# 8 KB runs in the expert weight loads, and the next expert's token count read to registers in mid-expert

## The chip, the cores and the metric

The kernel runs on one core of one Trainium2 chip. The metric is the device time of one execution in microseconds (us). All times below are of that one core; a profiled execution also leaves a span, from its first instruction to its last.

## The reference

One layer of an encoder on 256 tokens of width 1024, in float32: an attention and recurrent mixer with input and output projections, then a mixture of 32 experts of which each token uses 4, then a final norm. Nearly all the weights are the experts': three matrices of 1024 by 1024 each, 12 MB per expert, 403 MB in all. Cut to the experts:

```python
logits = (xf @ w_router + b_router)
top_v, top_i = lax.top_k(logits, 4)
gates = jax.nn.softmax(top_v)
# for each expert e, for the tokens that chose it:
g = xb @ w_gate[e] + b_gate[e]
u = xb @ w_up[e] + b_up[e]
g = jnp.minimum(g, 7.0)
u = jnp.clip(u, -7.0, 7.0)
y = ((u + 1.0) * (g * sigmoid(1.702 * g))) @ w_down[e] + b_down[e]
out[token] += gate * y
```

## The kernel before, in words

The front part (attention, recurrence, output projection, router) takes the first 149 us. It leaves for every token and expert a position in that expert's list (`pos`), a gate, and for every expert the number of its tokens (`cnti`).

Then a loop over 32 experts, written out. One expert handles up to 64 of its tokens in a block: its x columns are gathered and transposed to `xT`, `ffn1` multiplies them by `w_gate` (into PSUM tile `pg`) and `w_up` (`pu`), the activation follows on VectorE (DVE) and ScalarE (ACT), `h_trans` transposes the hidden activations, and `ffn2` multiplies by `w_down` (`pu`). With only 64 rows, two matmuls (`h` or `q` of 0 and 1) run side by side in the two column halves of TensorE. Gather of the next expert and scatter of the last pair lie between these stages. TensorE's instruction stream is called PE, its weight loads PEld, and what its sequencer handles alone PEq.

Should an expert have more than 64 tokens, `overflow` runs further blocks (`ov_block`) ahead of the normal one, nested up to three deep, each behind a branch on the count. The count must be in a register of PE, DVE and ACT for that: `load_cnt(e)` (line 994) reads it with `TENSOR_LOAD`, and on PE also computes and issues a `BRANCH_PREFETCH_HINT` for the branch. In the loop it stands right behind the branch of expert e and reads the count of e + 1. Where an `If` is skipped, each engine's sequencer runs an `EVENT_SEMAPHORE` (line 928), which on PE waits until all matmuls ahead have ended.

Weights come in chunks of 1 MB: 256 rows of a matrix, two rows (k = 0, 1) for each of 128 partitions, 4 KB each from two places 512 KB apart. Four chunks make a matrix, twelve an expert. `prefetch` (line 165) issues them all from SyncE (SP, line 173) in the order of use into a ring of 21 slots (`RING`), so SP runs ahead until it has to wait for a slot. A chunk's slot comes free when the last matmul on it has ended.

Of the kernel before, what the change touches and what calls it, by code (L numbers as in the profile page):

```python
# [18 lines left out]
ET = mybir.EngineType  # L19
# [4 lines left out]
KC = D // 128  # L24
# [15 lines left out]
def rope_table():  # L40
# [8 lines left out]


COLS = [("norm1_g", 8), ("conv_w", 16), ("conv_b", 4), ("lru_ba", 8), ("lru_bi", 8), ("lru_lam", 8),
        ("norm2_g", 8), ("attn_out_g", 4), ("lru_out_g", 4)]
OFF = {n: sum(c for _, c in COLS[:i]) for i, (n, _) in enumerate(COLS)}
NCOL = sum(c for _, c in COLS)


def packs(a):

    cols = np.concatenate([np.asarray(a[n]).reshape(c, 128) for n, c in COLS]).T
    rope = rope_table().reshape(NT, 128, 2 * HD).transpose(1, 0, 2).reshape(128, -1)  # L60
    heads = [np.broadcast_to(np.asarray(a[n]).reshape(1, HD), (128, HD)) for n in ("q_norm_g", "k_norm_g")]
    lru = [np.asarray(a[n])[0].reshape(2, LC, 2, 64, 64).transpose(2, 3, 0, 1, 4).reshape(128, -1)
           for n in ("lru_wa", "lru_wi")]
    wr = np.asarray(a["w_router"])[0].reshape(KC, 128, E).transpose(1, 0, 2).reshape(128, -1)
    br = np.broadcast_to(np.asarray(a["b_router"]).reshape(1, E), (128, E))
    return {"pack_a": np.ascontiguousarray(cols),
            "pack_b": np.ascontiguousarray(np.concatenate([rope] + heads + lru, 1)),
            "pack_c": np.ascontiguousarray(np.concatenate([wr, br], 1))}


def bc(ap, shape):
    return ap.to_broadcast(shape)


def body(ctx, tc, A, out):
    nc = tc.nc
    V, S, G, PE = nc.vector, nc.scalar, nc.gpsimd, nc.tensor
# [80 lines left out]


    w_out_d = A["w_out"][0].rearrange("(c k p) n -> c p k n", k=2, p=128)  # L160
    srcs = [A[n][0].rearrange("e (c k p) n -> e c p k n", k=2, p=128) for n in ("w_gate", "w_up", "w_down")]
    plan = [("o", 0, c) for c in (0, 1, 2, 3)] + [(m, e, c) for e in range(E) for m in range(3) for c in range(4)]
    loaded = {}

# [681 lines left out]
def experts(tc, A, out, g):  # L846
# [5 lines left out]
    with ExitStack() as ctx:  # L852
# [3 lines left out]
        Y = [wk.tile([128, 512], F32, name=f"Y{d}") for d in range(2)]  # L856
        xo = wk.tile([128, KC, 64], F32, name="xo")
        gTo = wk.tile([128, NT, 128], F32, name="gTo")
        n2 = bc(pcols("norm2_g", KC).rearrange("p (h c) -> p c h", h=2)[:, :, :, None], [128, 4, 2, 64])

        ssf = wk.tile([128, NT, 2], F32, name="ssf")

# [9 lines left out]
        def gather(sl):  # L872
# [6 lines left out]
            S.activation(xr, p, AF.Copy)  # L879
            return xr  # L880

        def gather_trans(xr, dst):
            p = ps([128, 4, 2, 64])
            for c in range(4):
                PE.transpose(p[:, c].rearrange("p a b -> p (a b)"), xr[:, c * 128:(c + 1) * 128], ident)  # L885
            V.tensor_tensor(dst.rearrange("p (h c) s -> p c h s", h=2), p, n2, OP.mult)  # L886

        def ffn1(w, xT, e, which, tag="pu"):
# [10 lines left out]
        def act_gate(p, gp):  # L899
            sg = wk.tile([128, 512], F32, name="sg", tag="sg")  # L900
            V.tensor_scalar(gp, p, LIMIT, None, op0=OP.min)  # L901
            S.activation(sg, gp, AF.Sigmoid, scale=ALPHA)  # L902
            V.tensor_tensor(gp, gp, sg, OP.mult)
# [6 lines left out]
        def h_trans(h, hT):  # L910
            p = ps([128, 4, 128])
            for c in range(4):
                PE.transpose(p[:, c, :], h[:, c * 128:(c + 1) * 128], ident)  # L913
            S.activation(hT, p.rearrange("p a b -> p (a b)"), AF.Copy)

        def ffn2(w, hT, flip):
# [8 lines left out]

        def overflow(cnt, e, w, b=1):

            with tc.If(cnt > 64 * b, preferred_fallthrough_block=True, label=f"ov{e}" if b == 1 else None):  # L928
                ov_block(e, b, *w)
                if b < 3:  # L930
                    overflow(cnt, e, w, b + 1)
# [61 lines left out]

        def load_cnt(e):
            c = nc.values_load(cnti[:, e:e + 1], engines=(ET.PE, ET.DVE, ET.Activation), min_val=0, max_val=T)
            tc.mark_branch_hint_location(f"ov{e}", (c + 191) >> 8, engines=(ET.PE,))
            return c

        def ov_block(e, b, wg, wu, wd):
            gather_trans(gather(select(e, b)), xo)  # L1000
# [10 lines left out]
        xr = gather(sl)  # L1011
# [5 lines left out]
        for e in range(E):  # L1017
            last = e == E - 1
            wg, wu, wd = weights(0, e), weights(1, e), weights(2, e)
            overflow(cnt, e, (wg, wu, wd))  # L1020
            if not last:
                cnt = load_cnt(e + 1)
            gp = wk.tile([128, 512], F32, name="gp")
            if e >= E - 2:
                gd = one_pick(e, 0, "gd")
            elif e % 2 == 1:
                gd = combine(e)
            if not last:
                sl = select(e + 1, 0)
            pg = ffn1(wg, xT, e, 0, "pg")  # L1030
            act_gate(pg, gp)
            if last:
                one_scatter(g0, Y[0], False, (0,))
                one_scatter(g0, Y[0], False, (1,), (0,))
                g1 = wk.tile([128, NT, 2, 128], F32, name="gT", tag="gT")[:, :, 0]
                one_weights(g1, gd)
            act_up(ffn1(wu, xT, e, 1), gp)
            if e == E - 2:
                g1 = wk.tile([128, NT, 128], F32, name="g1")
                one_weights(g1, gd)  # L1040
            elif e % 2 == 1 and not last:
                gT = pair_weights(gd)
            if not last:
                xr = gather(sl)
            hT = wk.tile([128, 512], F32, name="gd", tag="gd")
            h_trans(gp, hT)
            if last:
                one_scatter(g0, Y[0], False, (1,), (1,))
            else:
                xT = wk.tile([128, KC, 64], F32, name="xT")  # L1050
                gather_trans(xr, xT)
            if e % 2 == 0 and e > 0:
                pair_scatter(gT, False)
            if e == 2:
                add_b_down()
            if e < E - 2:
                py = ffn2(wd, hT, e % 2)
                for q in range(2):
                    S.activation(Y[q ^ (e % 2)][q * 64:q * 64 + 64, :], py[q * 64:q * 64 + 64, :], AF.Copy)  # L1059
            else:  # L1060
                S.activation(Y[e % 2], ffn2(wd, hT, 0), AF.Copy)  # L1061
            if e == E - 2:
                g0 = g1
                fgs = slot([128, NT, D])
                fgb, fgrow = fgs[:, 0], fgs[0:KC, 1, 0:128]
                nc.gpsimd.dma_start(fgrow, A["final_g"].rearrange("(n p) -> n p", p=128))  # L1066
                for h in range(2):
                    p = ps([128, 4, 128])
                    for c in range(4):
                        k = h * 4 + c  # L1070
                        PE.matmul(p[:, c, :], lhsT=bc(ident[0:KC, k:k + 1], [KC, 128]), rhs=fgrow,
                                  start=True, stop=True)
                    V.tensor_copy(fgb[:, h * 512:(h + 1) * 512], p.rearrange("p a b -> p (a b)"))
# [46 lines left out]
```

## Time and profile before

| | |
|---|---|
| time, median of 3 runs | 1143.39 us (1140.66 to 1144.08) |
| profiled execution, its time | 1146.21 us |
| its span | 1144.5 us |
| PE busy | 1040.8 us, 91% of the span |
| HBM read | 416.54 MB, 365 GB/s over the span |
| granted TensorE clock, mean | 0.970 of full speed |

The profiled execution took 1.7 us beyond its span, and 2.8 us more than the median of the runs. PE busy counts every matmul from start to modelled end, and matmuls overlap, so 91% says that PE seldom stood still, not that it ran at its peak. Both PE and the transfers from HBM are busy most of the time, so the averages alone don't tell which one sets the end.

### The profile page before, as it was taken

Reading aid. Unit: us, or ns where it says so; the run is one execution under the profiler, and the core shown is the slowest. Engines: PE = TensorE matmul, PEld = TensorE weight load, DVE = VectorE, ACT = ScalarE, POOL = GpSimd, SP = SyncE. Lnnn points to the kernel's source line nnn. Section 1 sums busy time; section 2 is a strip of 40 time slices with the busy share of each in tenths; the row PEclk is TensorE's granted clock in tenths of the full one; section 3 lists DMA queues with packets and bytes.
Section 4 is the critical chain, followed back from the end, with each engine's and each line's share of the span. In section 5 each row is a group of like instructions: output and inputs, shape, how many; then the busy total and the mean of one; then the engine's idle time right before and its main releaser. Section 6 shows DMA issues by size and latency. Waiting matters only on the chain. (4 is left out here: it accounts for less than half of the span.)

```text
span 1144.5 us, 12376 instructions
## 1 busy us (share of the span) xinstructions
PE 1040.8 (91%) x4886; PEld 413.1 (36%) x4886; DVE 277.0 (24%) x601; ACT 190.2 (17%) x341; POOL 67.0 (6%) x54
## 2 busy tenths in 40 slices
PE   7877989999899899987999999799999999999995
PEld 6664533333333333322333333233333333333331
DVE  8797412111112111210112121021211111212121
ACT  4745511111111111110011111011111111111112
POOL 5554200000000000000000000000000000000000
PEclk9889989999999999997999999899999999999998
DMA  9456769999999999996999999399999999999993
GB/s 322 188 200 251 284 249 403 409 408 409 408 409 408 409 408 409 408 409 243 391 408 408 409 408 409 139 394 410 407 409 408 408 408 409 408 409 408 408 409 147
DMA packets 114144, 419.14 MB, mean 366 GB/s; under 512 B 6664, under 2 KB 13968, under 8 KB 114032
## 3 DMA queue, kind: packets, MB, share of 16 engines
q1 hardware_dynamic: 113856, 417.21, 92.4%
q8 instruction: 74, 1.21, 0.4%
q0 software_dynamic: 176, 0.40, 0.1%
q14 instruction: 38, 0.31, 0.1%
HBM read 416.54 MB, written 1.05 MB: 365 GB/s over the span
## 5 line engine op out<-in xcount | busy, mean ns | idle before, releaser
L895 PE MATMUL pg<-w,xT 128*64 128x512 f32 x1024 | 234.3, 611 | 0.0
L922 PE MATMUL pu<-w,gd 128*64 128x512 f32 x1024 | 228.5, 599 | 0.0
L895 PE MATMUL pu<-w,xT 128*64 128x512 f32 x1024 | 225.4, 592 | 0.0
L895 PEld LDWEIGHTS pg<-w,xT 128*64 128x64 f32 x1024 | 78.0, 141 | 135.6 <-issue 131.5
L895 PEld LDWEIGHTS pu<-w,xT 128*64 128x64 f32 x1024 | 75.7, 137 | 138.0 <-issue 130.3
L922 PEld LDWEIGHTS pu<-w,gd 128*64 128x64 f32 x1024 | 71.1, 137 | 144.1 <-issue 136.7
L901 DVE TENSOR_SCALAR gp<-pg 128x512 f32<-128x512 f32 x32 | 22.1, 692 | 338.9 <-PE pg L895 338.9
L1059 ACT ACTIVATE Y<-pu 64x512 f32<-64x512 f32 x60 | 35.5, 592 | 271.9 <-PE pu L922 271.5
L902 ACT ACTIVATE sg<-gp 128x512 f32<-128x512 f32 x32 | 20.1, 629 | 287.8 <-DVE gp L901 287.8
L865 DVE TENSOR_SCALAR gd<-iota,pos,gates 128x64 f32<-128x64 f32 x128 | 30.1, 309 | 153.5 <-PEq L928 143.5
L907 DVE TENSOR_SCALAR sg<-pu 128x512 f32<-128x512 f32 x34 | 23.5, 692 | 161.0 <-PE pu L895 160.8
L876 PE MATMUL pt<-x,sr 128*64 128x512 f32 x256 | 61.3, 599 | 0.0
L891 PE MATMUL pg<-b,emask 96*64 96x512 bf16 x68 | 14.7, 427 | 49.4 <-issue 25.1
L973 PE MATMUL ps<-Y,gT 128*128 128x512 f32 x120 | 54.0, 592 | 0.0
L1066 POOL DMA_DIRECT2D w<-in_final_g_dram x1 | 0.5, 523 | 868.2 <-DMA w<-in_w_down_dram 868.2
L879 ACT ACTIVATE sg<-pt 128x512 f32<-128x512 f32 x34 | 20.3, 597 | 138.4 <-PE pt L876 138.4
L891 PEld LDWEIGHTS <-emask 96*64 96x64 bf16 x136 | 8.1, 109 | 85.7 <-issue 78.8
L886 DVE TENSOR_TENSOR xT<-pt,prm 128x512 f32<-128x512 f32 x32 | 22.1, 692 | 67.8 <-PE pt L885 67.8
L695 PE MATMUL ps<-w 128*128 128x512 f32 x64 | 30.2, 623 | 4.9 <-DVE w L571 4.9
L973 PEld LDWEIGHTS ps<-Y,gT 128*128 128x128 f32 x120 | 21.6, 190 | 21.5 <-issue 21.5
L885 PE MATMUL pt<-ident,sg 128*128 128x128 f32 x136 | 22.2, 286 | 6.4 <-ACT sg L879 6.3
L876 PEld LDWEIGHTS pt<-x,sr 128*64 128x64 f32 x256 | 17.2, 136 | 29.9 <-issue 25.4
(282 smaller groups left out, 768.3 us busy)
## 6 DMA issues: line engine op xcount, KB each, us to landing
w<-in_w_gate_dram SPq DMA_DIRECT2D x128, 1024.0 KB, 18.4
w<-in_w_up_dram SPq DMA_DIRECT2D x128, 1024.0 KB, 18.4
w<-in_w_down_dram SPq DMA_DIRECT2D x127, 1024.0 KB, 18.3
w<-in_w_in_dram SPq DMA_DIRECT2D x6, 1024.0 KB, 13.1
w<-in_w_out_dram SPq DMA_DIRECT2D x4, 1024.0 KB, 7.5
x<-in_x_dram SPq DMA_DIRECT2D x2, 512.0 KB, 3.9
w<-in_w_in_dram SPq DMA_DIRECT2D x2, 512.0 KB, 6.6
w<-in_w_down_dram SPq DMA_DIRECT2D x2, 512.0 KB, 17.6
```

The costliest lines, as they stand in the source:

```text
L695: PE.matmul(p, lhsT=mT[:, kk, t * 128:(t + 1) * 128], rhs=wo[kk // 2][:, kk % 2, d * 512:(d + 1) * 512], start=k == 0, stop=k == 3)
L865: V.tensor_scalar(dst[:, t], iota[:, b], pos[:, t, e:e + 1], weight[:, t], op0=OP.is_equal, op1=OP.mult)
L876: PE.matmul(p[h * 64:h * 64 + 64, :], lhsT=sl[:, t, :], rhs=x1[:, t, h * 512:(h + 1) * 512], start=t == 0, stop=t == NT - 1)
L885: PE.transpose(p[:, c].rearrange("p a b -> p (a b)"), xr[:, c * 128:(c + 1) * 128], ident)
L886: V.tensor_tensor(dst.rearrange("p (h c) s -> p c h s", h=2), p, n2, OP.mult)
L891: PE.matmul(p[h * 64:h * 64 + 64, :], lhsT=bc(emask[:, e:e + 1], [96, 64]), rhs=b3[:, which, h * 512:(h + 1) * 512], start=True, stop=False)
L895: PE.matmul(p[h * 64:h * 64 + 64, :], lhsT=xT[:, k, :], rhs=w[k // 2][:, k % 2, h * 512:(h + 1) * 512], start=False, stop=k == KC - 1)
L901: V.tensor_scalar(gp, p, LIMIT, None, op0=OP.min)
L907: V.tensor_scalar(u, p, LIMIT, -LIMIT, op0=OP.min, op1=OP.max)
L922: PE.matmul(p[q * 64:q * 64 + 64, :], lhsT=hT[:, c * 128 + hf * 64:c * 128 + hf * 64 + 64], rhs=w[j // 2][:, j % 2, d * 512:(d + 1) * 512] ...
L973: PE.matmul(acc[t][d], lhsT=gT[:, t, d, :], rhs=Y[d], start=False, stop=last)
L1059: S.activation(Y[q ^ (e % 2)][q * 64:q * 64 + 64, :], py[q * 64:q * 64 + 64, :], AF.Copy)
```

## The change

Two changes go together. First, the weight chunks of `w_gate`, `w_up` and `w_down` are cut so that one partition's two rows are neighbours in HBM: one run of 8 KB in place of two of 4 KB. Partition p of a chunk then holds rows 2p and 2p + 1, no longer p and 128 + p. So the transposes that feed these matmuls (`gather_trans`, `h_trans`) take every second column (`column_pairs`), and the norm's gains get a second copy in that order (`norm2_p`). Second, `load_cnt(e + 1)` moves behind the first `ffn1` of expert e. With it, each of the nested overflow branches gets a prefetch hint of its own, issued at the start of the block ahead of it; before, only the first had one.

```diff
 COLS = [...
-        ("norm2_g", 8), ("attn_out_g", 4), ("lru_out_g", 4)]
+        ("norm2_g", 8), ("attn_out_g", 4), ("lru_out_g", 4), ("norm2_p", 8)]
...
+    pairs = np.asarray(a["norm2_g"]).reshape(4, 128, 2).transpose(0, 2, 1)
...
-    srcs = [A[n][0].rearrange("e (c k p) n -> e c p k n", k=2, p=128) for n in ("w_gate", "w_up", "w_down")]
+    srcs = [A[n][0].rearrange("e (c p k) n -> e c p k n", k=2, p=128) for n in ("w_gate", "w_up", "w_down")]
...
+        def column_pairs(a, c):
+
+            return a[:, c // 2 * 256 + c % 2:(c // 2 + 1) * 256:2]
+
         def gather_trans(xr, dst):
...
-                PE.transpose(p[:, c].rearrange("p a b -> p (a b)"), xr[:, c * 128:(c + 1) * 128], ident)
+                PE.transpose(p[:, c].rearrange("p a b -> p (a b)"), column_pairs(xr, c), ident)
...
         def h_trans(h, hT):
...
-                PE.transpose(p[:, c, :], h[:, c * 128:(c + 1) * 128], ident)
+                PE.transpose(p[:, c, :], column_pairs(h, c), ident)
...
-            with tc.If(cnt > 64 * b, preferred_fallthrough_block=True, label=f"ov{e}" if b == 1 else None):
+            with tc.If(cnt > 64 * b, preferred_fallthrough_block=True, label=f"ov{e}_{b}"):
+                if b < 3:
+                    hint(cnt, e, b + 1)
                 ov_block(e, b, *w)
...
         def load_cnt(e):
             c = nc.values_load(cnti[:, e:e + 1], engines=(ET.PE, ET.DVE, ET.Activation), min_val=0, max_val=T)
-            tc.mark_branch_hint_location(f"ov{e}", (c + 191) >> 8, engines=(ET.PE,))
+            hint(c, e, 1)
             return c
+
+        def hint(c, e, b):
+
+            tc.mark_branch_hint_location(f"ov{e}_{b}", (c + 255 - 64 * b) >> 8, engines=(ET.PE,))
...
             overflow(cnt, e, (wg, wu, wd))
-            if not last:
-                cnt = load_cnt(e + 1)
...
             pg = ffn1(wg, xT, e, 0, "pg")
+            if not last:
+                cnt = load_cnt(e + 1)
             act_gate(pg, gp)
```

On PE, at the end of an expert's overflow branches, before the change (the rows `ISA` are register operations of the count and the hint; `pg` and `pu` are the first products):

```order
L928 UNCONDITIONAL_BRANCH x4
L995 TENSOR_LOAD cnti
L995 ISA x2
L996 ISA
L1116 BRANCH_PREFETCH_HINT
L891 LDWEIGHTS emask
L891 MATMUL pg<-b_78,emask 64x512
L891 LDWEIGHTS emask
L891 MATMUL pg<-b_78,emask 64x512
L895 MATMUL pg<-w,xT 64x512 x16
L891 LDWEIGHTS emask
L891 MATMUL pu<-b_78,emask 64x512
```

The same place with the change:

```order
L933 UNCONDITIONAL_BRANCH x4
L896 LDWEIGHTS emask
L896 MATMUL pg<-b_78,emask 64x512
L896 LDWEIGHTS emask
L896 MATMUL pg<-b_78,emask 64x512
L900 MATMUL pg<-w,xT 64x512 x16
L1002 TENSOR_LOAD cnti
L1002 ISA x2
L1008 ISA
L1127 BRANCH_PREFETCH_HINT
L896 LDWEIGHTS emask
L896 MATMUL pu<-b_78,emask 64x512
```

The load, its register operations and the hint have moved from ahead of the `pg` matmuls to behind them.

On PE, at the start of an overflow block, with the change:

```order
L927 MATMUL pu<-w,gd 64x512 x16
L933 COMPARE_AND_BRANCH
L1008 ISA
L1127 BRANCH_PREFETCH_HINT
L877 MATMUL pt<-x_68,sro 64x512 x4
L890 MATMUL pt<-ident,sg 128x128 x4
```

The two rows between the branch and the block's first matmul are new: the hint for the next nested branch.

On SP, the weight loads around one of the branches, before the change:

```order
L173 DMA w<-in_w_down_dram 128x2x1024 x4
L173 DMA w<-in_w_gate_dram 128x2x1024
L928 UNCONDITIONAL_BRANCH
L173 DMA w<-in_w_gate_dram 128x2x1024 x3
L173 DMA w<-in_w_up_dram 128x2x1024 x4
```

And with the change:

```order
L174 DMA w<-in_w_down_dram 128x2048 x4
L174 DMA w<-in_w_gate_dram 128x2048
L933 UNCONDITIONAL_BRANCH
L174 DMA w<-in_w_gate_dram 128x2048 x3
L174 DMA w<-in_w_up_dram 128x2048 x4
```

The order and number of loads is unchanged; each now names 128 runs of 2048 elements, where it named 256 of 1024.

## Rows read from the trace of the kernel before

**Rows 1.** The page: the span, and the DMA rate in 40 slices.

```profile
span 1144.5 us, 12376 instructions
...
GB/s 322 188 200 251 284 249 403 409 408 409 408 409 408 409 408 409 408 409 243 391 408 408 409 408 409 139 394 410 407 409 408 408 408 409 408 409 408 408 409 147
```

**Rows 2.** Busy by stretch (us, then busy by engine, clock, DMA share, GB/s): two experts.

```profile
563.60:589.90 26.30, 25.08 (x120) 8.83 (x120) 5.29 (x13) 3.44 (x7) 0.00 (x0) 1.00 1.02 410
589.90:619.00 29.10, 27.77 (x124) 9.86 (x124) 4.43 (x10) 3.00 (x6) 0.00 (x0) 1.00 1.03 408
```

**Rows 3.** SP in order of time, around the second overflow block.

```profile
709.29 35.10 SPq L173 DMA_DIRECT2D w<-in_w_down_dram  x3
742.31 3.80 SPq L173 DMA_DIRECT2D w<-in_w_down_dram  x3
```

**Rows 4.** PEld in order of time, expert 30, third and fourth chunk of w_up.

```profile
1084.34 0.15 PEld L895 LDWEIGHTS pu<-w,xT 128*64 128x64 f32 x2 [0.28 <-issue]
1085.26 0.20 PEld L895 LDWEIGHTS pu<-w,xT 128*64 128x64 f32 x4 [0.77 <-DMA w<-in_w_up_dram]
```

**Rows 5.** PE in order of time, the boundary before an even expert.

```profile
589.98 0.41 PE L891 MATMUL pg<-b,emask 96*64 96x512 bf16 x2 [1.11 <-PEq L928]
```

**Rows 6.** Sequencer instructions of lines 928, 995, 996, 1116: ns min/median/max.

```profile
L928 PEldq COMPARE_BRANCH  x36: 90/3364/6090, 144.4 to 1101.2; - x36
L928 PEldq EVENT_SEMAPHORE  x32: 51/51/51, 148.0 to 1103.3; - x32
L995 PEldq TENSOR_LOAD <-cnti x32: 302/306/493, 143.2 to 1071.8; - x32
L995 PEldq FUSED_REGOPS  x32: 157/157/171, 143.8 to 1072.2; - x32
L995 PEldq SEQ_ASSERT  x32: 18/18/24, 144.1 to 1072.4; - x32
L996 PEldq FUSED_REGOPS  x32: 59/59/65, 144.1 to 1072.5; - x32
L1116 PEldq BRANCH_PREFETCH_HINT  x32: 35/35/53, 144.3 to 1072.6; - x32
```

**Rows 7.** Line 891 from 149 to 739 us: pu's first matmul, sequencer's event.

```profile
L891 PE MATMUL pu<-b,emask x40: 381/382/383, 159.0 to 710.5; 96*64 96x512 bf16 x40
L891 PEldq EVENT_SEMAPHORE  x18: 51/51/51, 154.8 to 677.2; - x18
```

**Rows 8.** DMA from 742 to 1126 us: all packets, queue 1.

```profile
DMA packets 40065, 154.69 MB, mean 403 GB/s; under 512 B 2390, under 2 KB 2398, under 8 KB 40024
...
q1 hardware_dynamic: 39992, 154.13, 100.7%
```

**Rows 9.** DMA from 5 to 11 us, loads of 1 KB rows.

```profile
DMA packets 1974, 2.09 MB, mean 348 GB/s; under 512 B 48, under 2 KB 1936, under 8 KB 1974
...
q1 hardware_dynamic: 1974, 2.09, 104.1%
```

**Rows 10.** PE in order of time, behind the two overflow blocks.

```profile
532.17 0.64 PE L891 MATMUL pg<-b,emask 96*64 96x512 bf16 x2 [5.14 <-issue]
...
738.60 0.64 PE L891 MATMUL pg<-b,emask 96*64 96x512 bf16 x2 [3.14 <-issue]
```

**Rows 11.** Line 928 from 524 to 533 and from 733 to 739 us.

```profile
L928 PEldq COMPARE_BRANCH  x2: 197/2936/5675, 525.1 to 530.9; - x2
...
L928 PEldq COMPARE_BRANCH  x2: 187/1937/3687, 733.5 to 737.4; - x2
```

**Rows 12.** Busy by stretch behind the overflow blocks; the clock is third from the end.

```profile
530.10:537.00 6.90, 4.83 (x14) 1.57 (x16) 0.00 (x0) 0.00 (x0) 0.00 (x0) 0.51 0.01 2
...
738.30:741.80 3.50, 3.20 (x10) 1.18 (x12) 0.00 (x0) 0.00 (x0) 0.00 (x0) 0.51 0.00 0
```

**Rows 13.** Groups of PEld, 563.6 to 589.9 us: a transpose's weight loads.

```profile
L913 PEld LDWEIGHTS pt<-ident,gp 128*128 128x128 f32 x4 | 0.4, 140 | 0.8 <-issue 0.8
```

**Rows 14.** PE in order of time, the boundary with the slow branch, 379 us.

```profile
379.65 0.41 PE L891 MATMUL pg<-b,emask 96*64 96x512 bf16 x2 [2.75 <-PEq L928]
```

More of the change, by code (lines that the diff above doesn't have):

```diff
@@ L57, in packs @@
 def packs(a):
-    cols = np.concatenate([np.asarray(a[n]).reshape(c, 128) for n, c in COLS]).T
+    pairs = np.asarray(a["norm2_g"]).reshape(4, 128, 2).transpose(0, 2, 1)
+    cols = np.concatenate([np.asarray(pairs if n == "norm2_p" else a[n]).reshape(c, 128) for n, c in COLS]).T
     rope = rope_table().reshape(NT, 128, 2 * HD).transpose(1, 0, 2).reshape(128, -1)
@@ L858, in experts @@
         gTo = wk.tile([128, NT, 128], F32, name="gTo")
-        n2 = bc(pcols("norm2_g", KC).rearrange("p (h c) -> p c h", h=2)[:, :, :, None], [128, 4, 2, 64])
+        n2 = bc(pcols("norm2_p", KC).rearrange("p (h c) -> p c h", h=2)[:, :, :, None], [128, 4, 2, 64])
         ssf = wk.tile([128, NT, 2], F32, name="ssf")
```

## The prediction

> **What bounds the kernel now.** I read the DMA rate by slices first. From 149 us on it stands at 408 GB/s, except in two dips around 530 and 730 us and at the end [rows 1]. That looks like a kernel bound by its weight transfers, but the stretches of single experts say otherwise: an odd expert takes PE 26.3 us and an even one 29.1, with 25.08 and 27.77 us busy [rows 2]. A pair takes 55.4 us, 27.7 an expert. In that time the transfers bring 408 x 27.7 = 11.3 MB (of 10^6 bytes), where an expert needs twelve chunks of 1.0486, 12.58 MB. So PE eats weights faster than they come, and lives on the lead of the 21-slot ring. An overflow block gives the lead back: it uses weights already there for some 25 us more, the ring fills, and SP waits (the stretch of 35.10 us on SP that ends when it goes on at 742.31 [rows 3]). In the whole loop I find PE held up by a weight at one place: in expert 30, up's fourth chunk, its weight load came after 0.77 us of idle time released by the DMA, where 0.28 is usual [rows 4]. The lead is used up there, and half a microsecond was lost.
>
> So the kernel has two parts. Up to 742 us PE sets the pace, with lead to spare, and what PE saves arrives in full, because the stopped transfers start again that much sooner. From 742 to about 1126 us PE and the transfers finish together to within 0.5 us, and what PE saves there is worth only what the transfers save too.
>
> **The moved count.** In each boundary PE stands idle 1.11 us before the next expert's first matmul, released by its own sequencer [rows 5]. That gap holds the event that waits for the last matmul (51 ns), the TENSOR_LOAD (306), two register operations (157 and 59), an assertion (18) and the hint (35): 626 ns in instructions, the other half us in six steps from one to the next [rows 6]. The change leaves the event and two steps, some 0.14 us, so I take 0.97 off each boundary. At the least the moved instructions' own 575 ns go, at the most all of 1.11. Of the 32 loads one stays ahead of the loop and 31 move, one in each expert but the last. By 711 us `pu` had been started 40 / 2 = 20 times [rows 7], two of them for overflow blocks, so 18 experts were past, and the 19th has its load behind the second overflow block, just ahead of 738.6. That leaves 12 for the time after it.
>
> At its new place the sequence has about 0.9 us of PE's sequencer. The cover is the matmuls queued ahead: at this place the sequencer already handles an event of its own, the first at 154.8 us, and the matmul behind it starts at 159.0 [rows 7]. So the sequencer is 4.2 us ahead, and I cost the move at nothing. Were there no such lead, each would cost its 0.97 us again and the change would bring nothing. On DVE the load goes behind the picks, seven us ahead of `pg`; on ACT it keeps its place. What is late next at the boundary is the matmul drain itself.
>
> Worth: 19 x 0.97 = 18.4 us up to 742, in full; up to 12 x 0.97 = 11.6 behind it, if the transfers keep up.
>
> **The 8 KB runs.** No row has 8 KB rows on this queue, so I bound them. From 742 to 1126 us, queue 1 moved 154.13 MB in 39,992 packets at 100.7% of 16 engines [rows 8]: 1.007 x 16 x 384 = 6187 us, and without the 2,390 tiny ones 164.5 ns per 4 KB. In the front, 1,974 packets of nearly all 1 KB took 104.1% of 16 x 6 us [rows 9], 50.6 ns for 1,059 bytes in the mean. A line through both has 0.0375 ns per byte and 10.9 ns per packet. 8 KB in one packet would take 318 ns, in place of 329: 3.4% less. The other bound is nothing, since the 4 KB packets may be held by bytes alone; and a loss I exclude as longer runs gained in these rows (348 to 408 GB/s). Between them I take the middle, 1.7%, as two rows can't part a cost per packet from what else differs between the front and the loop. Over 384 us that is 6.5 us. The Trainium skill (DMA: Bandwidth & Descriptors, Why small descriptors are slow) states a fixed cost of about 3 cycles per packet at 32 bytes a cycle. By that, 4 KB take 131 cycles and 8 KB 259, a gain of 1.1%, or 4.3 us, an estimate from that page, nearer to no gain than the rows' line is.
>
> So behind 742 us PE could save 11.6 and the transfers save 6.5. They set the end: 6.5 us count, and PE waits out some 5.
>
> **The nested hints.** After each overflow block a second branch, unhinted before, took 5675 and 3687 ns in the sequencer [rows 11], and PE stood 5.14 and 3.14 us [rows 10]. Around and behind these idle spells the clock was granted at half (0.51, the 1.2 GHz level) for 6.9 and 3.5 us [rows 12]. PE was busy 4.83 and 3.20 us of that, work that takes half as long at the full clock: 4.0 us together. If the hint makes these branches short (the shortest are of 90 ns, the median of all 3364 [rows 6]), the two gaps, 8.3 us together, shrink to some 0.4 each; 7.5 us less, of which 1.9 are counted above. So this gives 0 to 5.5 + 4 = 9.5 us. As the first branches have a hint and half of them still take over 3.3 us, I take a third, 3 us. Both stalls lie ahead of 742 and count in full.
>
> **Columns by pairs.** Eight weight loads per expert now step over every second element. They take 140 ns now [rows 13]; no row shows a step of two in one. I take no cost; as the other end, twice the time, 8 x 0.14 = 1.1 us per expert. The Trainium skill (SBUF — State Buffer, Door 1: The DMA port swizzle) says that two float32 in one 16-byte line are enough for full rate, which would make it free; no run here shows it yet. Eight more columns of gains ride in a load ahead of everything and cost nothing.
>
> **The sum.** 1144.5 - 18.4 - 6.5 - 3 = 1116.6 us of span, 1118.3 of time in a profiled execution (1.7 beyond the span). The runs' median was 2.8 below the profiled one, so 1115.5; I say 1116.
>
> **The rivals.** *No gain from 8 KB.* Engines are already busy 100.7% [rows 8]; if bytes alone hold them, the end follows the transfers as they are: 1144.5 - 18.4 - 3, or 1122 as a median. Against it: the longer rows in rows 9 and 8 are cheaper per byte.
>
> *PE is the bound throughout.* If 8 KB gain 3% or more, PE's 11.6 us come through: 1144.5 - 30.1 - 3 = 1111.4, or 1110; with the nested hints at their best, 1104. For it: the line through both rows says 3.4%.
>
> *The strided weight loads take it back.* At 1.1 us per expert PE loses 35 us and gains 30 and the 3 of the hints: 1144.5 + 5 - 3, or 1145 as a median, no change by the 0.3% (3.4 us) that a measurement can tell, or a little slower. Against it: a transpose's weight load of 140 ns has a matmul beside it.
>
> *Slower: the branch's fetch.* A branch takes 3.4 us in the median and 6.09 at the most [rows 6], hidden by the same lead of 4.2 us; the one at 379 us came out of it and left PE 2.75 idle, 1.64 over the usual [rows 14]. The hint now comes a quarter expert nearer to its branch. If that makes every fetch a long one, 31 x 1.64 = 51 us come on top and 30 go: 1165 or so. It is slower from 18 such branches on (30.1 / 1.64); before there were two in 31. Against it: two thirds of an expert lie between hint and branch still, 26.3 x 2 / 3 = 17.5 us, almost three times the longest fetch. The Trainium skill (Runtime: NRT & Kernel Launch, Instruction fetch mechanics) says that a taken branch outside the window forces a fetch before execution goes on; by that rule, these branches would stall whatever the hint says, and nested ones keep 3.7 to 5.7 us.
>
> **How the numbers follow.** The forecast, with between 0.8 and 2.8% from the runs: 0.48. No gain from 8 KB: 0.20. PE bound throughout: 0.18. Strided loads: 0.06. Fetches: 0.05. The rest (such as a boundary that gives only 0.57 us; 19 x 0.57 = 10.9 and no DMA gain give 1132): 0.03. The time is the likeliest one's, whose own range is 1111 to 1120. For 8 in 10 the range takes in both neighbours, from 1104 (PE bound, nested hints at their best) to 1129 (no DMA gain, no nested gain, 0.8 us per boundary: 1144.5 - 15.2 - 1.1 = 1128). Faster: 0.48 + 0.20 + 0.18 and the rest, 0.89. Within 0.3%: most of the strided case, 0.04. Slower: 0.07.
>
> **What would show it.** Right: the gap ahead of an expert's first matmul near 0.15 us; TENSOR_LOAD on PE between `pg` and `pu` with no idle PE there; DMA at some 415 GB/s in the slices; SP's long wait ending some 20 us earlier than 742; weight loads released by DMA in the last ten experts, and few before. Wrong: gaps of 1 us at the new place, transposes above 0.7 us for four, more boundaries of 2 us and more, or a DMA rate that is below 400 with the ring never full.

## The result, and the profile after

The changed kernel took 1102.51 us in the median of four runs (1101.89 to 1111.59), the kernel before 1143.74 beside it: a ratio of 0.9658, with an interval of 0.9603 to 0.9714. A second set of six runs of the same kernel gave 1105.1 against 1146.13, 0.9649 (0.9623 to 0.9675). That is 41 us less, where 27 were forecast; the time lies 1.5 us under the low end of the forecast's range in the first set and 1.1 above it in the second. So the direction was forecast, and the gain came out at one and a half times its forecast size.

The profiled execution has a span of 1100.5 us. The page shows the DMA rate in the loop at 420 GB/s, where it was 408 [rows 1]:

```profile
span 1100.5 us, 12380 instructions
...
GB/s 325 179 218 248 243 269 415 420 420 420 420 420 420 420 420 420 420 422 419 416 420 420 420 420 421 214 390 420 419 420 420 420 420 421 419 421 420 419 420 134
```

Busy time by stretch, for the same two experts as in [rows 2] (from the start of one's first matmul to that of the next):

```profile
535.92:561.40 25.48, 25.25 (x120) 9.72 (x121) 6.27 (x17) 3.60 (x7) 0.00 (x0) 1.00 1.01 422
561.40:589.57 28.17, 27.95 (x124) 10.79 (x125) 3.49 (x6) 3.01 (x6) 0.00 (x0) 1.00 1.01 420
```

They take 0.82 and 0.93 us less than before, although PE is busy 0.17 and 0.18 us longer in them. PE in order of time shows both halves of that: the boundary behind the first overflow block, an ordinary boundary, and the one behind the second overflow block (idle time before the matmul in brackets; 5.14, 1.11 and 3.14 before [rows 10, 5]):

```profile
507.74 0.41 PE L896 MATMUL pg<-b,emask 96*64 96x512 bf16 x2 [0.46 <-PEq L933]
...
561.40 0.41 PE L896 MATMUL pg<-b,emask 96*64 96x512 bf16 x2 [0.16 <-PEq L933]
...
705.08 0.41 PE L896 MATMUL pg<-b,emask 96*64 96x512 bf16 x2 [0.46 <-PEq L933]
```

and the groups of PEld and PE in the odd expert show what the columns by pairs cost: a transpose's weight load takes 208 ns (140 before [rows 13]) and its matmul 308.

```profile
L918 PE MATMUL pt<-ident,gp 128*128 128x128 f32 x4 | 0.7, 308 | 0.0
...
L918 PEld LDWEIGHTS pt<-ident,gp 128*128 128x128 f32 x4 | 0.6, 208 | 0.8 <-issue 0.8
L890 PEld LDWEIGHTS pt<-ident,sg 128*128 128x128 f32 x4 | 0.6, 208 | 0.3 <-ACT sg L880 0.3
```

The branches (line 933 now) answer to [rows 6, 11]: over the whole program, behind the first overflow block, and behind the second. Columns are ns, smallest, median and largest. The nested ones fell from 5675 and 3687 ns to 447 and 346, and the median of all from 3364 to 367.

```profile
L933 PEldq COMPARE_BRANCH  x36: 90/367/3476, 144.3 to 1058.1; - x36
...
L933 PEldq COMPARE_BRANCH  x2: 197/322/447, 505.3 to 507.5; - x2
...
L933 PEldq COMPARE_BRANCH  x2: 200/273/346, 702.6 to 704.8; - x2
```

SP's long wait at the second overflow block ends when it goes on at 707.25 us, 35 earlier than the 742.31 of [rows 3]:

```profile
707.25 3.76 SPq L174 DMA_DIRECT2D w<-in_w_down_dram  x3
```

Near the end, PE waits for transfers in expert 30, now for three of the four chunks of w_up, where [rows 4] show one short wait:

```profile
1037.07 1.94 PE L900 MATMUL pu<-w,xT 128*64 128x512 f32 x8 [0.56 <-DMA w<-in_w_up_dram]
1039.54 1.94 PE L900 MATMUL pu<-w,xT 128*64 128x512 f32 x8 [0.54 <-DMA w<-in_w_up_dram]
1042.03 1.94 PE L900 MATMUL pu<-w,xT 128*64 128x512 f32 x8 [0.55 <-DMA w<-in_w_up_dram]
```

The point that splits the program is the start of expert 18's ordinary block, right behind the second overflow block, since the transfers restart 2 to 4 us later. It came at 738.60 us before and comes at 705.08 now: 33.5 us were gained ahead of it. Behind it 1144.5 - 738.6 = 405.9 us became 1100.5 - 705.1 = 395.4: 10.5 more. All kernels below are read at this point.

### The profile page after: what moved, and what is told of

Its sections match the earlier page's. It is cut to its first block, busy times and chain, and to the rows that moved or that the text cites. A ratio compares the mean times of both kernels' runs of the same rounds, so it can differ in the third digit from the quotient of the medians.

```text
span 1100.5 us, 12380 instructions
## 1 busy us (share of the span) xinstructions
PE 1037.2 (94%) x4886; PEld 435.2 (40%) x4886; DVE 276.9 (25%) x601; ACT 192.3 (17%) x341; POOL 67.1 (6%) x54
## 5 line engine op out<-in xcount | busy, mean ns | idle before, releaser
L900 PE MATMUL pg<-w,xT 128*64 128x512 f32 x1024 | 227.5, 595 | 0.2 <-issue 0.2
L900 PEld LDWEIGHTS pu<-w,xT 128*64 128x64 f32 x1024 | 82.8, 137 | 133.4 <-issue 122.8
L900 PEld LDWEIGHTS pg<-w,xT 128*64 128x64 f32 x1024 | 83.8, 137 | 122.6 <-issue 117.4
L918 PEld LDWEIGHTS pt<-ident,gp 128*128 128x128 f32 x128 | 17.8, 208 | 27.6 <-DVE gp L913 14.6
L890 PE MATMUL pt<-ident,sg 128*128 128x128 f32 x136 | 25.2, 308 | 3.6 <-ACT sg L880 1.5
L908 DVE TENSOR_TENSOR gp<-gp,sg 128x512 f32<-128x512 f32 x32 | 22.2, 693 | 24.2 <-ACT sg L907 24.2
```

The source lines that it names most:

```text
L890: PE.transpose(p[:, c].rearrange("p a b -> p (a b)"), column_pairs(xr, c), ident)
L900: PE.matmul(p[h * 64:h * 64 + 64, :], lhsT=xT[:, k, :], rhs=w[k // 2][:, k % 2, h * 512:(h + 1) * 512], start=False, stop=k == KC - 1)
```

## The experiments

The theory after the result: the moved count is worth what was forecast; the nested hints are worth far more, because a slow branch leaves PE idle and often a half-clock stretch behind; and the 8 KB runs are worth more too, but only where PE is fast enough to wait for transfers. The rivals: all of it comes from the 8 KB runs; or the hints act only by shifting the code.

All kernels in one table: the median, its ratio to the kernel before in the same session with the interval, and of the profiled execution the start of expert 18's ordinary block (in PE's order of time), the rest of the span, and the span. The kernel before took 1144.86 us beside the first four, 1144.65 beside the next four (from "all but nested hints" on) and 1146.13 beside the last three.

| kernel | us | ratio | expert 18 at | rest | span |
|---|---|---|---|---|---|
| before | 1144.86 | 1 | 738.6 | 405.9 | 1144.5 |
| 8 KB runs alone | 1144.76 | 1.0005 (0.9988 to 1.0022) | 730.7 | 405.2 | 1135.9 |
| moved count alone | 1125.43 | 0.9834 (0.9808 to 0.9860) | 716.2 | 406.7 | 1122.9 |
| nested hints alone | 1129.82 | 0.9871 (0.9849 to 0.9893) | 724.7 | 403.7 | 1128.4 |
| moved count + nested hints | 1117.15 | 0.9760 (0.9738 to 0.9782) | 711.8 | 404.4 | 1116.2 |
| all but nested hints | 1118.95 | 0.9775 (0.9743 to 0.9807) | 718.0 | 398.0 | 1116.0 |
| all, nested hints wrong | 1113.51 | 0.9742 (0.9711 to 0.9773) | 713.8 | 397.3 | 1111.1 |
| all, contiguous columns | 1107.67 | 0.9663 (0.9638 to 0.9689) | 707.9 | 398.3 | 1106.2 |
| all, pairs made by ACT and DVE | 1104.90 | 0.9647 (0.9624 to 0.9669) | 706.7 | 398.4 | 1105.1 |
| the same again | 1105.53 | 0.9643 (0.9618 to 0.9668) | 702.8 | 397.1 | 1099.9 |
| all (the change) again | 1105.10 | 0.9649 (0.9623 to 0.9675) | 705.2 | 396.1 | 1101.3 |
| moved count + 8 KB, no hint at all | 1285.94 | 1.1225 (1.1191 to 1.1258) | 812.5 | 470.6 | 1283.1 |

**8 KB runs alone.** The weights' layout, the column pairs and `norm2_p` as in the change; the count is loaded behind the overflow block, and only the first branch has a hint.

```
-    srcs = [A[n][0].rearrange("e (c k p) n -> e c p k n", k=2, p=128) for n in ("w_gate", "w_up", "w_down")]
+    srcs = [A[n][0].rearrange("e (c p k) n -> e c p k n", k=2, p=128) for n in ("w_gate", "w_up", "w_down")]
...
-                PE.transpose(p[:, c, :], h[:, c * 128:(c + 1) * 128], ident)
+                PE.transpose(p[:, c, :], column_pairs(h, c), ident)
```

> 8 KB runs and the column pairs alone; the count's load and the single hint stay where they were before. First theory (the parts act apart: 8 KB speeds the transfers, the hints shorten the branches): the DMA slices read 420 GB/s, but PE is the bound throughout, so this gains nothing; the strided weight loads cost 0.18 us per expert, slow branches of 3 us and more stay at about 18 of 36, the gaps of 5.1 and 3.1 us behind the overflow blocks stay: span 1147 to 1151. Rival (the branches' fetches were slow because the 4 KB transfers crowded them out): few branches above 1 us, both gaps below 2 us, span near 1132.

Measured: no change (1.0005). The transfers do run faster, 420 GB/s against 410 and 408 in [rows 2], but PE waits for no chunk; busy time by stretch, of the even expert 14, has PE busy 27.95 of 29.19 us:

```profile
582.25:611.44 29.19, 27.95 (x125) 10.07 (x126) 4.51 (x10) 3.07 (x6) 0.00 (x0) 1.00 1.01 420
```

So the gain doesn't come from the 8 KB runs by themselves. (The profiled run of this kernel is at the fast end of its own 1137.64 to 1147.74, so its 730.7 in the table is no gain. In it the branch behind the first overflow block took 3.82 us in place of 5.68 and left PE 3.23 idle in place of 5.14, with no hint changed: hints are not all that sets such a stall.)

**The moved count alone.**

```
             overflow(cnt, e, (wg, wu, wd))
-            if not last:
-                cnt = load_cnt(e + 1)
...
             pg = ffn1(wg, xT, e, 0, "pg")
+            if not last:
+                cnt = load_cnt(e + 1)
```

> The count's load moved alone; 4 KB runs, one hint. First theory: the gap ahead of an expert goes from 1.11 to 0.16 us, 19 x 0.95 = 18 us come through ahead of 742 us, and behind it the transfers at 408 GB/s set the end, so a span of 1125 to 1127 with PE waiting some 11 us for weights in the last experts; the gaps behind the overflow blocks stay at 4 and 2 us or more. Rival (the hint's later place makes the branches short): in addition few first branches above 1 us, no clock dips at 230 and 380 us, span near 1118.

Measured: 19.4 us less. PE in order of time: idle for 4.58 us behind the first overflow block, and for 0.16 at an ordinary boundary:

```profile
517.07 0.64 PE L891 MATMUL pg<-b,emask 96*64 96x512 bf16 x2 [4.58 <-PEq L928]
...
601.02 0.41 PE L891 MATMUL pg<-b,emask 96*64 96x512 bf16 x2 [0.16 <-PEq L928]
```

Up to expert 18 the kernel gains 22.4 us, behind it nothing (406.7 against 405.9): with 4 KB runs PE then waits for transfers instead.

**The nested hints alone.**

```
-            with tc.If(cnt > 64 * b, preferred_fallthrough_block=True, label=f"ov{e}" if b == 1 else None):
+            with tc.If(cnt > 64 * b, preferred_fallthrough_block=True, label=f"ov{e}_{b}"):
+                if b < 3:
+                    hint(cnt, e, b + 1)
```

> The nested hints alone; 4 KB runs, load where it was before. First theory (the nested hint makes the branch behind an overflow block short, 0.45 us in place of 5.7 and 3.7): the two gaps fall to about 1.4 us each, the half-clock stretches behind them go, 9.5 us in all: span near 1135. Rival (the short branches came from the load's new place or from the 8 KB runs): gaps as before, span 1143 to 1146.

Measured: 15.0 us less, five times the forecast's 3 and beyond its bound of 9.5. Behind the overflow blocks PE, in order of time, idles 1.42 and 1.37 us, in place of the 5.14 and 3.14 of [rows 10]:

```profile
523.65 0.41 PE L891 MATMUL pg<-b,emask 96*64 96x512 bf16 x2 [1.42 <-issue]
...
724.72 0.41 PE L891 MATMUL pg<-b,emask 96*64 96x512 bf16 x2 [1.37 <-issue]
```

The bound had left out that two ordinary boundaries change as well, those of 2.85 and 2.75 us before (of experts 5 and 8; the latter is [rows 14]): here they show 1.17 and 1.11.

**Both, with 4 KB runs.** The two diffs above together.

> Load moved and nested hints, 4 KB runs, plain columns. First theory: 18 us of the moved load and 9.5 of the hints come through ahead of the second overflow block's end, the transfers at 408 GB/s set the rest: span 1115 to 1118, PE waiting 10 us or more for weights in the last experts. Rival (8 KB is needed for the short branches): span near 1125, gaps of 3 us and more behind the overflow blocks.

Measured: 1117.15, so 8 KB runs bring 12 to 15 us on top of the other two, where they bring nothing alone. PE in order of time shows what they remove: waits for two or more chunks of w_up in expert 11, in the first overflow block and in experts 28, 29 and 30, and for w_gate in expert 30. Expert 28:

```profile
987.40 1.94 PE L895 MATMUL pu<-w,xT 128*64 128x512 f32 x8 [0.41 <-DMA w<-in_w_up_dram]
989.96 1.94 PE L895 MATMUL pu<-w,xT 128*64 128x512 f32 x8 [0.62 <-DMA w<-in_w_up_dram]
992.55 1.94 PE L895 MATMUL pu<-w,xT 128*64 128x512 f32 x8 [0.66 <-DMA w<-in_w_up_dram]
995.11 1.94 PE L895 MATMUL pu<-w,xT 128*64 128x512 f32 x8 [0.62 <-DMA w<-in_w_up_dram]
```

**The change without the nested hints.** The nested branches lose hint and name; the rest of the change stays.

```
-            with tc.If(cnt > 64 * b, preferred_fallthrough_block=True, label=f"ov{e}_{b}"):
-                if b < 3:
-                    hint(cnt, e, b + 1)
+            with tc.If(cnt > 64 * b, preferred_fallthrough_block=True, label=f"ov{e}_1" if b == 1 else None):
```

> The changed kernel without the hints inside the overflow blocks (and without a name for the nested branches); the moved count and the 8 KB runs stay. Theory A, the hints inside the blocks are worth much more than the 3 us of the prediction, because a fetched branch leaves PE idle and the idle time is followed by a stretch at half clock: the kernel with the moved count alone took 1125.4 us and that with the hints as well 1117.2, 8.3 us less. Then the two nested branches take over 3.3 us again, the gaps behind the second and third overflow block are about 4.6 and 1.9 us (0.45 and 0.46 in the changed kernel), two ordinary boundaries show about 1.8 us (0.16), and half-clock stretches of 3 to 4 us follow the long gaps. Together some 11 to 13 us up to expert 18, of which the transfers' own limit at the end takes back a part: 1106 to 1112 us. Theory B, as predicted: only the nested fetch itself, about 3 us: 1104 to 1106. Theory C, the hints do nothing and the changed kernel's shorter gaps come from the earlier count: 1101 to 1103, gaps of about 0.5 us.

(What this calls the second and third block are the first and second that run.) Measured: 1118.95, 14 to 16 us more than the change and beyond even theory A. PE in order of time shows a gap of 1.84 us at an ordinary boundary again, and of 4.40 behind the first overflow block; the ordinary one's branch and one other took 6.11 and 6.06 us:

```profile
289.17 0.41 PE L896 MATMUL pg<-b,emask 96*64 96x512 bf16 x2 [1.84 <-PEq L933]
...
516.87 0.64 PE L896 MATMUL pg<-b,emask 96*64 96x512 bf16 x2 [4.40 <-PEq L933]
```

No overflow block has run by 289 us, so no nested hint has been carried out there in any kernel. What differs from the change at this place is only the code in the skipped blocks. It doesn't set that branch alone: in the kernel with 8 KB runs alone, which has no nested hints either, the branch took 4.39 us and the boundary shows the usual 1.12. Why these two branches are slow stays open.

**The change with its nested hints wrong.** Every instruction is that of the change; one constant makes the nested hints always name the way into the next block, which neither of the two blocks takes.

```
-                    hint(cnt, e, b + 1)
+                    hint(cnt, e, b + 1, 255)
...
-            tc.mark_branch_hint_location(f"ov{e}_{b}", (c + 255 - 64 * b) >> 8, engines=(ET.PE,))
+            tc.mark_branch_hint_location(f"ov{e}_{b}", (c + (k or 255 - 64 * b)) >> 8, engines=(ET.PE,))
```

> The changed kernel, instruction for instruction, with one constant different: the hints inside the overflow blocks always name the way into the next block, which is the wrong one in both of the blocks that run without a further one. It tells the two ways in which those hints could act. Theory A, the hint names the way that the branch then takes, and saves its fetch: with the wrong way the nested branches take over 3.3 us again (447 and 346 ns in the changed kernel), the gaps behind the two blocks are 2 to 5 us, and half-clock stretches follow: 1104 to 1108 us, while the ordinary branches of experts 13 to 31 stay at 0.35 to 0.45 us. Theory B, the gain comes from where the code lies (some instructions more in each expert's block shift all that follows): nothing changes, nested branches under 0.5 us, 1101 to 1103 us. Theory C, a wrong hint also spoils the later branches, as the unhinted nested branch seems to in the kernel before (3.1 to 3.7 us in each of experts 14 to 18, against 0.35 to 0.46 in the changed kernel): these take over 3 us again, which the queue ahead of PE hides.

Measured: 1113.51, 8 to 11 us more than the change. The nested branches took 6194 and 3437 ns, as long as without a hint (5907 and 3347 in the run above; line 933 around the two blocks, ns):

```profile
L933 PEldq COMPARE_BRANCH  x2: 197/3196/6194, 506.0 to 512.4; - x2
...
L933 PEldq COMPARE_BRANCH  x2: 190/1814/3437, 709.9 to 713.6; - x2
```

The gaps behind the blocks, of PE in order of time, are 4.69 and 1.93 us:

```profile
512.62 0.64 PE L896 MATMUL pg<-b,emask 96*64 96x512 bf16 x2 [4.69 <-PEq L933]
...
713.83 0.41 PE L896 MATMUL pg<-b,emask 96*64 96x512 bf16 x2 [1.93 <-PEq L933]
```

Behind the first one the clock was granted at half for 5 us (0.51, third from the end in this stretch's row):

```profile
512.50:517.50 5.00, 4.88 (x14) 1.60 (x16) 0.00 (x0) 0.00 (x0) 0.00 (x0) 0.51 0.65 269
```

The ordinary boundaries of experts 1 to 30 stay at 0.16 us, and the branches from expert 15 on at 0.35 to 0.38: theories B and C fall, and theory A holds but for its time, which was too low. So the two last runs split the nested hints' worth. Naming the right way makes the two branches short and saves the half clock behind them, 8 to 11 us. The rest of the 14 to 16, some 5, goes with the presence of the hints' code and not with what they say: 3.3 us of it are the idle time at two ordinary boundaries (1.84 and 1.79 in place of 0.16).

**Contiguous columns.** `column_pairs` returns `a[:, c * 128:(c + 1) * 128]`; the experts' weights then meet the wrong columns of x and h, and only the time is of interest.

> The changed kernel with contiguous columns in the eight transposes of an expert, so that the weights of the experts meet the wrong columns of x and h; everything else as it is. It measures the price of the strided columns, which the prediction set to nothing. Theory A, each transpose waits for its longer weight load (208 ns against 140): PE's busy time of an expert falls by 0.18 us, loads at 140 ns; up to expert 18 that is 19 x 0.18 = 3.4 us, two or three tenths more for the overflow blocks, and behind it, where the transfers set the end, little: 1097 to 1099 us. Theory B, the longer load lies beside other matmuls: busy time as before, 1101 to 1103 us.

Measured: PE's busy time falls by 0.18 us in an expert, as theory A says, but its idle time grows by 0.09, and an expert takes 25.40 and 28.09 us in place of 25.48 and 28.17. The median, 1107.67, is no lower than the change's, against both theories.

**The pairs made elsewhere.** A version with the right columns, meant to beat the change: ACT's eviction of the gathered rows and DVE's product of h read every second element and write even and odd columns apart.

```
-            S.activation(xr, p, AF.Copy)
+            S.activation(split(xr), pairs(p), AF.Copy)
...
+            at = c % 2 * 256 + c // 2 * 128
+            return a[:, at:at + 128]
...
-            V.scalar_tensor_tensor(gp, u, 1.0, gp, op0=OP.add, op1=OP.mult)
+            V.scalar_tensor_tensor(split(hp), pairs(u), 1.0, pairs(gp), op0=OP.add, op1=OP.mult)
```

Here `pairs` views columns as "p (m k) -> p k m" and `split` as "p (k m) -> p k m", with k = 2.

> The changed kernel with the pairing of columns moved from TensorE's weight loads to the operations that write the tiles: ACT's eviction of the gathered rows and DVE's last product of h read every second element and write even and odd columns apart, so that the eight transposes read contiguous columns. Theory A, a stride costs these two engines nothing (692 and 599 ns stay) and the weight loads fall to 140 ns: as without a stride, 1097 to 1099 us. Theory B, the stride makes the product of h longer by some tenth of a us, and the transposes of h wait for just that product (PE idle 0.07 us before them): 1101 to 1104 us, no gain. Theory C, a strided read costs a multiple there: 0.7 us more in each expert on PE's path, over 1115 us.

Measured: the stride is free on DVE (692 ns, as before), and weight loads are at 141 ns (groups of one odd expert):

```profile
L923 DVE SCALAR_TENSOR_TENSOR hp<-sg,gp 128x512 f32<-128x512 f32 x1 | 0.7, 692 | 0.0
...
L929 PEld LDWEIGHTS pt<-ident,hp 128*128 128x128 f32 x4 | 0.4, 141 | 0.8 <-issue 0.8
```

Yet the time was 1104.9. Experts are shorter by 0.09 us, but the profiled execution met half clock once more than the change's, in expert 2. So both were run again together.

> The kernel with the pairing moved to ACT and DVE once more, unaltered. Theory A, its shorter expert (25.39 and 28.08 us against 25.48 and 28.18) is worth 19 x 0.09 = 1.7 us or more and the first result was hurt by half-clock stretches that come and go: 1100 to 1102 us, below the changed kernel. Theory B, nothing is left of the 1.7 us, since the transfers set the end of the program: the same as the changed kernel within 2 us.

> The changed kernel once more, unaltered, beside the kernel with the pairing moved to ACT and DVE, since their difference (1102.5 against 1104.9 us, from separate sets of runs) is smaller than the spread of either: 1102 to 1104 us. If the half-clock stretches fall at the same places in the program each time, the profile shows none near 230 us; if they come and go, a stretch of 3.3 us near 230 us, as in the kernel with the pairing moved, may show here too.

Measured: 1105.53 and 1105.10, the same; theory B. The stretch of expert 2, in this kernel's first profile and in its second, shows that the half clock comes and goes (clock 0.90 and 1.00; 3.4 us between them). The two profiles are of two chips, but the six runs of the second set, on one chip, show it too: two took 1101.35 and 1101.60 us at a mean granted clock of 0.980, four took 1105.41 to 1107.15 at 0.975 or 0.976. The change's second profile has no such stretch in expert 2, and its own ten runs spread over 1101.89 to 1111.59:

```profile
200.00:235.90 35.90, 35.06 (x136) 12.92 (x137) 3.94 (x7) 3.00 (x6) 0.00 (x0) 0.90 1.01 420
```

```profile
199.70:232.20 32.50, 31.69 (x134) 12.27 (x134) 3.87 (x6) 2.94 (x6) 0.00 (x0) 1.00 1.01 420
```

In the second, PE reaches expert 30 at 1023.68 us, 3.5 before the change's second profile, but now waits for gate's chunks too and ends only 1.4 us earlier:

```profile
1027.93 1.94 PE L909 MATMUL pg<-w,xT 128*64 128x512 f32 x8 [0.42 <-DMA w<-in_w_gate_dram]
1030.41 1.94 PE L909 MATMUL pg<-w,xT 128*64 128x512 f32 x8 [0.54 <-DMA w<-in_w_gate_dram]
```

**No hint at all.** The change without the first hint of each expert and without the nested ones.

> The changed kernel without any hint, the first one of each expert left out too, so that the worth of hints as such is seen. Theory A, every branch fetches its way in 3 to 6 us, and those of the experts without an overflow block lie beside the 4.2 us that the queue runs ahead: the branches of experts 12 to 31 are over 3 us again, boundaries show 0.2 to 2.5 us where a branch takes over 4 us, and the kernel is a few us slower than that without the hints inside the blocks (1119.0 us): 1119 to 1135 us. Theory B, only the branches into an overflow block matter: as without the hints inside the blocks, 1115 to 1121 us.

Measured: 1285.94, far beyond both theories. Neither had reckoned with a second wait in each expert. A branch takes 6.07 us in the median (line 933 over the whole program, ns):

```profile
L933 PEldq COMPARE_BRANCH  x36: 82/6069/6790, 142.8 to 1238.3; - x36
```

PE in order of time idles 1.89 us at this ordinary boundary, and once more, 2.65 us, some matmuls into the expert, released by nothing but its own issue:

```profile
878.81 0.41 PE L896 MATMUL pg<-b,emask 96*64 96x512 bf16 x2 [1.89 <-PEq L933]
...
884.42 3.76 PE L900 MATMUL pg<-w,xT 128*64 128x512 f32 x10 [2.65 <-issue]
```

PE's waits over the whole program (us in total, times, longest) show that this is so in nearly every expert:

```profile
PE pg L900 <- issue: 75.9, 28, 3.9
PE pg L896 <- PEq L933: 58.0, 29, 4.1
```

That is 134 us; with the clock's stretches behind them (mean granted clock 0.951, against 0.981) the kernel loses 181 us against the change beside it, 5.7 for each of 32 experts. What PE waits for the second time isn't shown.

## Why the prediction was right, and where its sizes failed

**Two parts, PE ahead of the second overflow block and the transfers behind it: right, but by less than forecast.** With 4 KB runs every kernel takes 404 to 407 us behind it, whatever PE saves. With 8 KB runs and the earlier count it takes 395 to 398. PE was to wait out some 5 us there; in expert 30 it loses some 2.5 (its products with w_up take 9.8 us in place of 7.3), and the forecast's sign of "weight loads released by DMA in the last ten experts" came in that one alone. "With lead to spare" held only for the old PE: with the count moved, expert 11 and the first overflow block wait for 4 KB transfers as well.

**The moved count: right.** 0.97 us per boundary was forecast and 1.11 - 0.16 = 0.95 measured; 19 x 0.95 = 18.1 us. (The "some 0.14 us" that were to stay are less than the prediction's own terms, 51 ns and two of six steps of 81: 0.21; 0.16 was measured.) At the new place nothing shows, with PE idle 0.07 us in a whole odd expert.

**The 8 KB runs: right mechanism, mis-sized.** Forecast were 1.7% and 6.5 us behind 742 us; measured are 10.5 us there. Of these 8 KB runs are worth 9.0 (404.4 against 395.4 in the table, with count and hints the same; 8.3 by the change's second profile). The other 1.5 are a half-clock stretch that is gone: SP goes on 3.7 us behind expert 18's start before and 2.2 now. The price per packet can be taken as in the prediction, from 720 to 970 us. With 8 KB runs, in the change:

```profile
DMA packets 14290, 104.22 MB, mean 417 GB/s; under 512 B 1586, under 2 KB 1586, under 8 KB 1586
...
q1 hardware_dynamic: 14262, 103.85, 100.2%
```

and with 4 KB runs, in the kernel with the moved count and the nested hints:

```profile
DMA packets 26343, 101.83 MB, mean 407 GB/s; under 512 B 1551, under 2 KB 1551, under 8 KB 26314
...
q1 hardware_dynamic: 26314, 101.44, 101.8%
```

16 x 250 x 1.002 / (14262 - 1586) = 316 ns per 8 KB; 16 x 250 x 1.018 / (26314 - 1551) = 164.4 per 4 KB, twice that 329. The line through [rows 8, 9] had said 318. The failing step is "Between them I take the middle": the price per packet follows the rows' own line, the rate of the transfers rose by 2.9% (408 to 420 GB/s), and the middle gave some 2 us too little. Whether fewer packets do it, or that a partition reads from one place in HBM and no longer from two, no run separates. The Trainium skill (DMA: Bandwidth & Descriptors, Why small descriptors are slow) counts about 3 cycles per packet, by which 1.1% was estimated; the measured 3.9% per byte moved, or 2.9% in rate, differs from it, and the measurement decides. With it, the rival "PE is the bound throughout" came near: its 1104 with the nested hints at their best is what was measured, within 1.5 us. That is in part luck: PE still waits for transfers in expert 30, and the rival's sum has neither the strided loads nor the stalls and half-clock stretches outside the overflow blocks.

**The nested hints: the step that failed most.** "As the first branches have a hint and half of them still take over 3.3 us, I take a third, 3 us." Measured are 14 to 16. A right hint made both nested branches short (447 and 346 ns), and the first ones were long for a cause outside what the hints say: with the nested hints' code in place, even where it names the wrong way, none is above 0.5 us from expert 15 on. The bound of 9.5 us was what naming the right way brings (8 to 11); it lacked what the code's presence brings.

Ahead of expert 18, 33.5 us divide into 18.1 of the count; 8.28 - 0.92 = 7.4 of the two gaps behind overflow blocks, of which 1.9 are in the count; 1.7 each at two ordinary boundaries; and 6.5 that remain. These are half-clock stretches that are gone, less the strided loads. Busy time by stretch shows it for the blocks of expert 8 and of expert 12, before and with the change, and for all up to expert 18 (the clock is third from the end):

```profile
379.65:410.39 30.74, 29.47 (x125) 10.28 (x126) 4.45 (x10) 2.81 (x5) 0.00 (x0) 0.94 1.03 408
532.17:563.63 31.46, 30.13 (x126) 10.29 (x126) 4.51 (x10) 2.87 (x5) 0.00 (x0) 0.92 0.82 312
149.20:738.60 589.40, 544.37 (x2451) 192.29 (x2452) 97.97 (x221) 63.69 (x109) 0.57 (x1) 0.97 0.97 386
...
365.30:393.47 28.17, 27.95 (x124) 10.81 (x125) 3.50 (x6) 3.01 (x6) 0.00 (x0) 1.00 1.01 419
507.74:535.92 28.18, 27.94 (x125) 9.84 (x125) 3.50 (x6) 1.94 (x4) 0.00 (x0) 1.00 1.01 414
147.99:705.08 557.09, 539.90 (x2451) 204.31 (x2451) 98.01 (x221) 64.97 (x109) 0.57 (x1) 0.99 0.99 408
```

PE's busy time falls by 4.5 us there, though the strided loads add 0.18 in each of 20 blocks, 3.6 together; so some 8 us of it went with the half clock. Some of these stretches come and go, so not all of the 8 are the change's.

**Columns by pairs: not free, but nearly without effect.** No cost was taken; PE loses 0.18 us of busy time per expert and 0.09 of time, about 3 us over the program if nothing else set the end. The Trainium skill (SBUF — State Buffer, Door 1: The DMA port swizzle) has two float32 in a 16-byte line at full rate; for these weight loads the trace disagrees, 208 ns against 140. In the end the transfers hide it, as far as the runs can tell: with the loads back at 141 ns the median is the same.

**The slower rival: no.** With its hint a quarter expert nearer, no branch takes over 3.58 us in the change's two profiles. The Trainium skill (Runtime: NRT & Kernel Launch, Instruction fetch mechanics) says that a taken branch out of the fetched window waits for its code; the run without hints shows a wait at the branch, 6.07 us in the median, but not what it is for; and the nested branches show that a right hint removes it, where the prediction had taken from that rule that they would stall whatever the hint says. The page also has code fetched in blocks of 16 KiB, which could fit the two ordinary branches that changed with the code beside them; no run here moved code alone.

## What to carry to other kernels

Parts of a change don't add up where two limits lie close together: 8 KB runs gave nothing alone and 12 to 15 us once PE was faster (some 9 of them behind the last overflow block), so a part is to be judged on top of the others, not by itself. Where two rows give a line through a cost, the middle between it and nothing needs a reason of its own. And every branch on a busy engine deserves a hint that is right, the rare nested ones too: a slow branch costs its own gap and often the half clock behind it, and a wrong hint costs as much as none.

## What the runs showed that was not expected

Without any hint PE stalls twice in an expert, behind the branch and again some matmuls further, 5.7 us in all with the clock. With hints in code that had not been carried out, two ordinary branches took less time (6.1 us before; 0.44 and 2.9 with the change), though a run without those hints had one of them at 4.4. And of two executions of one kernel, one may hold a half-clock stretch of 3.4 us that the other lacks, with the same instructions; a difference of 2 us between two versions of this kernel can't be read from one profile of each. The change also leaves two half-clock stretches in the overflow blocks (0.59 and 0.52 of full speed on average), each behind 3.33 us in which PE stood idle and was released by DVE's sequencer:

```profile
495.80:500.00 4.20, 4.20 (x12) 1.27 (x14) 0.00 (x0) 0.00 (x0) 0.00 (x0) 0.59 1.01 415
690.50:697.60 7.10, 6.41 (x18) 2.25 (x20) 0.54 (x2) 0.60 (x1) 0.00 (x0) 0.52 0.64 270
```
